# Transposing 42 activation tiles by VectorE blocks and small transfers instead of TensorE, in a decoder layer on one Trainium2 core

## The chip, the core and the metric

The kernel runs on one core of one Trainium2 chip (trn2). The core's engines are TensorE (PE in the rows: matrix products and transposes, results in PSUM), VectorE (DVE), ScalarE (ACT), GpSimd (POOL) and SyncE (SP, which here only issues DMAs). The metric is the time on the device for one execution, in microseconds (us).

## The reference

One hybrid decoder layer and a last norm, in float32, on 256 tokens of width 2048; the inner width of the MLP is 5632.

```
h = rms_norm(x)
qa, ka, va, qb, kb, vb, ga, gb = split(h @ w_in)          # 1024 columns each, ga and gb 2048
oa = differential_attention(rope(qa), rope(ka), va)       # 8 heads, two softmax maps each
ob = stick_breaking_attention(qb, kb, vb)                 # 8 heads
m  = sigmoid(ga) * (oa @ w_proj_a) + sigmoid(gb) * (ob @ w_proj_b)
x  = x + m @ w_out
x  = x + cross_attention(rms_norm(x), rms_norm(mem))      # 4 heads, 256 memory tokens
u  = causal_conv3(rms_norm(x) @ w_up) + bias              # width 2 * 5632, a filter per column
x  = x + (silu(u[gate]) * u[value]) @ w_down
out = rms_norm(x)
```

## The kernel before

Every product is computed in units of 512 columns: x (256 tokens, two blocks of 128) times a [2048 x 512] piece of a weight matrix. The activations stand on TensorE's stationary side, so they are needed with features on the partitions, while a product comes out with tokens on the partitions. What a unit gives therefore has to be transposed before the next matrix can use it.

A weight piece comes from DRAM in four transfers of 1 MB, called b0 to b3 here (`product`, issued on SyncE; three buffers, pool `wr`). Each transfer is worked in two halves of two 128-row blocks, so a unit has halves 0 to 7. For each half ScalarE rounds the weights to a high part (`split_w`, the cast of line 162) and VectorE subtracts it to get the low part (line 163); three buffers each hold these parts. Each 128-row block then takes three matmuls of 128x512 per token block (lines 168, 169, 170: high times high, with the low part of the weights, with the low part of the activations), 12 matmuls a half and 96 a unit. SyncE waits before an issue until VectorE has read the buffer's last content.

Other work is put between the halves. A generator handed to `spawn(gen, delay)` starts `delay` halves later, and `tick()`, once a half, moves waiting generators on; a `yield n` lets n halves pass. SyncE's instructions stay in the order in which the program writes them (`manual_schedule`); on the other engines a scheduler sets the order.

The stages in order: the input projection in 20 units (qa0, ka0, va0, qa1, ka1, va1, then qb0, kb0, vb0, qb1, kb1, vb1, and eight gates), with the attention of a group of heads between the halves of later units; four times a unit of pa and one of pb (1024 rows each, so two transfers each), whose merged result is mT; four units of the output projection (wo, x1T); cross-attention (kx, qx, vx); four short units wxo (512 rows, one transfer each, x2T); 22 units up with the convolution and the gate between their halves; the down projection.

Transposes that the change touches are 42 sets of eight 128x128 transposes on TensorE against an identity, into PSUM. Eight are in `proj_T` (qaT, kaT, qbT, kbT, two of each; qa and ka are rotated on GpSimd first), four in mT, four in x1T, four in x2T (`transposed`), and 22 in `gated` (uT). In the up stage ScalarE scales the unit's two PSUM tiles into `zu` (line 588), and two halves later the transposes and the convolution follow.

Of the kernel before, what the change touches and what calls it, by code (L numbers as in the profile page):

```python
# [9 lines left out]
F32 = mybir.dt.float32  # L10
F32R = mybir.dt.float32r
AF = mybir.ActivationFunctionType
# [5 lines left out]
S = 256          # tokens  # L18
NT = S // P      # token blocks
D = 2048  # L20
KD = D // P      # 128-row blocks of the model width
FF = 5632
KF = FF // P
U = 512          # columns of one product unit
KB = 4           # 128-row blocks per weight transfer
# [6 lines left out]
# columns of the packed per-partition parameters  # L32
# [13 lines left out]
def hybrid_layer(ctx: ExitStack, tc: tile.TileContext, x, xT, mem, memT, gmix, par, gfin,  # L46
# [28 lines left out]
    # additive masks of the diagonal blocks: [q, k] -> 0 where k <= q (k < q), else NEG  # L75
# [8 lines left out]
    # Work that is emitted between the products: generators that yield the number of  # L84
    # half blocks of weights to let pass before they go on.
# [27 lines left out]
    def split(dst, src, gains=None):  # L113
        """dst[:, 0] + dst[:, 1] = src, or src * gain, in two parts of 12 bits.
        dst [P, 2, 2, S], src [P, 2, S]; gains: a [P, 1] column per 128-row block."""
        if gains is None:
            nc.scalar.copy(out=dst[:, 0], in_=src)
            nc.vector.tensor_tensor(out=dst[:, 1], in0=src, in1=dst[:, 0].bitcast(F32),
                                    op=ALU.subtract)
            return  # L120
        for j in range(2):
            nc.scalar.activation(out=dst[:, 0, j], in_=src[:, j], func=AF.Copy, scale=gains[j])
            nc.vector.scalar_tensor_tensor(out=dst[:, 1, j], in0=src[:, j], scalar=gains[j],
                                           in1=dst[:, 0, j].bitcast(F32),
                                           op0=ALU.mult, op1=ALU.subtract)

    def transposed(dst, src, n, name, gains=None):
        """dst: act tiles of the 4 row blocks n*4.. of the transpose; src [P, NT, U]."""
# [11 lines left out]

    def sumsq(dst, src):
        junk = wk.tile([P, U], F32, tag="w2", name="junk")
        nc.scalar.activation(out=junk[:, :src.shape[-1]], in_=src, func=AF.Square, accum_out=dst)

    def rstd(ss, n, width, name):
        """(sum over the last axis of ss [P, n, m] / width + EPS) ** -0.5 -> [P, n]"""
# [19 lines left out]
    def mm3(out, a, b, start=True, stop=True):  # L166
        """out (+)= (a[0] + a[1]).T @ (b[0] + b[1]) without the product of the two low parts."""
# [9 lines left out]
    def product(xs, w, u, kt_n, name, pieces=None, before=None, heap=False):  # L177
        """x @ w[:, unit u] for both token blocks -> two PSUM tiles [P, U].
        pieces: 128-row blocks per transfer; before(kt): called ahead of the transfer from kt on."""
# [25 lines left out]
    def load_split(src, gains, i, name):  # L205
        """Split act tile i of a transposed input [P, KD, S] in DRAM, scaled by gains."""
# [27 lines left out]
    def proj_T2(ps, r, name):  # L234
        """Evacuate a unit scaled by r and transpose it: act tiles of heads 0, 1 and 2, 3."""
# [7 lines left out]
    def proj_T(ps, r, name, rotate=False):  # L243
        """Evacuate a unit scaled by r and transpose it: [P (dim), 4 (head), S]."""
# [9 lines left out]
        def rest():  # L254
            for t in range(NT):
                pt = sm_tile(f"{name}_tp")
                for h in range(4):
                    nc.tensor.transpose(out=pt[:, h * P:(h + 1) * P],
                                        in_=zs[t][:, h * P:(h + 1) * P], identity=ident)
                nc.vector.tensor_copy(out=dst[:, :, t * P:(t + 1) * P],  # L260
                                      in_=pt.rearrange("p (h s) -> p h s", h=4))
            yield 0
        spawn(rest(), 2)
        return dst

    def proj_n(ps, r, name):
        """Evacuate a unit scaled by r: [P (token), NT, U]."""
# [5 lines left out]
    def attn_T(a, name):  # L273
        """Causal weights of one head [q block][P, K] -> [P (key), 3 * P]:
        keys 0 for both query blocks, then keys 1 for query block 1."""
# [8 lines left out]
    # differential attention  # L284
    oaT = [None] * 4

    def diff_head(h):
        qT, kT, v, hh = qa[h // 4], ka[h // 4], va[h // 4], h % 4
        # scores of the two maps, in a bank each: query block 0 in 0:P, query block 1 in P:3 * P
# [62 lines left out]
    # stick-breaking attention, two heads at a time  # L352
    obT = [None] * 4

    def stick_pair(g):
        aw = [[], []]
        for i in range(NT):
# [14 lines left out]
            # softplus(z) = max(z, 0) + ln(1 + exp(-|z|)), zero where masked  # L372
# [27 lines left out]
    # the input projection in units; the attention of a group of heads runs between the products  # L400
# [21 lines left out]
    # lam = exp(q1.k1) - exp(q2.k2) + LAM_INIT, negated, on all partitions  # L422
# [33 lines left out]
    # branch projections, gated and merged  # L456
    mT = [None] * 8
    for n in range(4):
# [9 lines left out]
        spawn(transposed(mT, ga, n, f"mT{n}"), 2)  # L468
# [6 lines left out]
    # output projection and residual  # L475
# [14 lines left out]
    for n in range(4):  # L490
# [4 lines left out]
        spawn(transposed(x1T, xr[n], n, f"x1T{n}", lambda k: col("g_x", k)), 2)  # L495
# [51 lines left out]
    for n in range(4):  # L547
        residual(product(oxT, w_xo, n, 4, f"wxo{n}"), xr[n], n, ss2)
        spawn(transposed(x2T, xr[n], n, f"x2T{n}", lambda k: col("g_ffn", k)), 2)
    r2 = rstd(ss2, NT, D, "r2")  # L550

# [1 line left out]
    gT = [None] * (KF // 2)  # L553

    def gated(i, z):
        us = []
        for part in range(2):          # gate, value
            pt = sm_tile("uT").rearrange("p (j s) -> p j s", j=2)
            for j in range(2):
                for t in range(NT):  # L560
                    c = (2 * part + j) * P
                    nc.tensor.transpose(out=pt[:, j, t * P:(t + 1) * P], in_=z[t][:, c:c + P],  # L562
                                        identity=ident)
            u = wk.tile([P, 2, S], F32, tag="w2", name="u")
            for j in range(2):
                f = part * KF + 2 * i + j
                tap = lambda k: col("cw", k * 2 * KF + f)
                nc.scalar.activation(out=u[:, j], in_=pt[:, j], func=AF.Identity, scale=tap(2),
                                     bias=col("cb", f))
                nc.vector.scalar_tensor_tensor(out=u[:, j, 1:], in0=pt[:, j, 0:S - 1], scalar=tap(1),  # L570
                                               in1=u[:, j, 1:], op0=ALU.mult, op1=ALU.add)
                nc.vector.scalar_tensor_tensor(out=u[:, j, 2:], in0=pt[:, j, 0:S - 2], scalar=tap(0),
# [11 lines left out]
    for i in range(KF // 2):  # L584
        ps = product(x2T, w_up, i, KD, f"up{i}")
        z = [wk.tile([P, U], F32, tag="w2", name=f"zu{t}") for t in range(NT)]
        for t in range(NT):
            nc.scalar.activation(out=z[t], in_=ps[t], func=AF.Copy, scale=r2[:, t:t + 1])
        spawn(gated(i, z), 2)
# [16 lines left out]
    def finish(ps, t):  # L606
        """The last unit's residual, the norm and the store of token block t."""
# [17 lines left out]
    # last unit: token block 0 runs ahead of token block 1, so that its end overlaps products  # L625
# [23 lines left out]
def _weight(w, np):  # L649
    """[K, N] -> [N / U, K / (KB * P), P, KB * U]: one contiguous transfer per block."""  # L650
# [5 lines left out]
def _tokens(a, np):  # L656
    """[S, D] -> [D / U, P, NT, U]"""
# [3 lines left out]
def _features(a, np):  # L661
    """[S, D] -> [P, KD, S]"""
# [49 lines left out]
```

## Time and profile before

| what | value |
|---|---|
| median of 3 runs | 1521.37 us (1520.65 to 1521.76) |
| span of the profiled execution | 1518.9 us |
| TensorE busy | 1503.4 us, 99% of the span |
| VectorE busy | 896.7 us, 59% |
| ScalarE busy | 784.7 us, 52% |
| GpSimd busy | 53.7 us, 4% |
| DMA, main queue | 286.13 MB, 54.5% of 16 engines' span |

The busy time of an engine is the sum over its instructions in one profiled execution; its share is taken of the span, the time from the first to the last instruction. The time of a run is a little longer than the span.

### The profile page before, as it was taken

To read this page: it belongs to the slowest core of one execution; us is meant where nothing else is said; L and a number is where in the kernel's file an instruction comes from. 1 tells how busy PE (TensorE), PEld (TensorE's weight loads), DVE (VectorE), ACT (ScalarE), POOL (GpSimd) and SP (SyncE) were. 2 spreads that over 40 slices of the span, in tenths; PEclk is the share of its full clock that TensorE was granted. 3 is DMA by queue.
4 is the path that set the end of the run, shared out by engine and by line. 5 is a ranking of instruction groups with operands and counts; after the bars stand their busy time and mean duration, and the time that the engine had idled before them with its cause. 6 is when DMAs were issued, how large, how long until landed. Compare 5 with 4: busy or idle time off the path is not lost.

```text
span 1518.9 us, 17599 instructions
## 1 busy us (share of the span) xinstructions
PE 1503.4 (99%) x6904; PEld 1243.2 (82%) x6904; DVE 896.7 (59%) x1131; ACT 784.7 (52%) x1074; POOL 53.7 (4%) x72
## 2 busy tenths in 40 slices
PE   8999999999999999999999999999999999999997
PEld 6878788888888888888888888888888888888886
DVE  5575666564444565664666667666666666444562
ACT  6454555465555344664565555555555555344441
POOL 0202000000000010000000000000000000000010
PEclk9999999999999999999999999999999999999999
DMA  9544444445555556755355555555555555655561
GB/s 349 187 159 152 162 166 167 167 166 194 194 194 193 183 193 246 265 197 192 139 191 174 189 194 178 183 194 185 179 191 192 174 190 192 222 194 192 197 230 73
DMA packets 44003, 287.78 MB, mean 189 GB/s; under 512 B 5008, under 2 KB 5008, under 8 KB 11152
## 3 DMA queue, kind: packets, MB, share of 16 engines
q1 hardware_dynamic: 43488, 286.13, 54.5%
q8 instruction: 54, 0.88, 0.2%
q10 hardware_dynamic: 432, 0.53, 0.1%
q14 instruction: 29, 0.24, 0.0%
HBM read 284.54 MB, written 2.10 MB: 189 GB/s over the span
## 4 chain that ended last, share of the span: by engine, by line
PE 98%; issue 1%; DMA 0%; DVE 0%; ACT 0%; SPq 0%; POOLq 0%; POOL 0%; DVEq 0%
PE up_mm L170 11%; PE up_mm L169 11%; PE up_mm L168 11%; PE dn_mm L168 5%; PE dn_mm L170 5%; PE dn_mm L169 5%; PE g_mm L168 4%; PE g_mm L169 4%; PE g_mm L170 4%; PE wo_mm L170 2%; PE wo_mm L168 2%; PE wo_mm L169 2%; PE uT L562 1%; PE va_mm L169 1%; PE qb_mm L169 1%; PE qb_mm L168 1%
## 5 line engine op out<-in xcount | busy, mean ns | idle before, releaser
L163 DVE TENSOR_TENSOR up_lo<-up_raw,up_hi 128x1024 fp32r<-128x1024 f32 x176 | 215.7, 1226 | 170.3 <-ACT up_hi L162 167.8
L162 ACT CAST up_hi<-up_raw 128x1024 fp32r<-128x1024 f32 x176 | 185.5, 1054 | 197.5 <-PE up_mm L170 176.5
L170 PE MATMUL up_mm<-up_hi,x2T 128*128 128x512 f32 x704 | 274.1, 389 | 0.0
L169 PE MATMUL up_mm<-up_lo,x2T 128*128 128x512 f32 x704 | 274.0, 389 | 0.0
L168 PE MATMUL up_mm<-up_hi,x2T 128*128 128x512 f32 x704 | 254.8, 392 | 0.0
L163 DVE TENSOR_TENSOR dn_lo<-dn_raw,dn_hi 128x1024 fp32r<-128x1024 f32 x88 | 109.9, 1253 | 101.0 <-ACT dn_hi L162 95.7
L170 PEld LDWEIGHTS up_mm<-up_hi,x2T 128*128 128x128 f32 x704 | 132.2, 188 | 27.4
L169 PEld LDWEIGHTS up_mm<-up_lo,x2T 128*128 128x128 f32 x704 | 132.3, 188 | 26.7
L168 PEld LDWEIGHTS up_mm<-up_hi,x2T 128*128 128x128 f32 x704 | 132.2, 188 | 26.6
L162 ACT CAST dn_hi<-dn_raw 128x1024 fp32r<-128x1024 f32 x88 | 92.0, 1056 | 118.0 <-PE dn_mm L170 103.7
L170 PE MATMUL dn_mm<-dn_hi,gT 128*128 128x512 f32 x352 | 136.9, 389 | 0.0
L169 PE MATMUL dn_mm<-dn_lo,gT 128*128 128x512 f32 x352 | 136.9, 389 | 0.0
L163 DVE TENSOR_TENSOR g_lo<-g_raw,g_hi 128x1024 fp32r<-128x1024 f32 x64 | 78.4, 1225 | 83.8 <-ACT g_hi L162 83.8
L168 PE MATMUL dn_mm<-dn_hi,gT 128*128 128x512 f32 x352 | 126.3, 389 | 0.0
L162 ACT CAST g_hi<-g_raw 128x1024 fp32r<-128x1024 f32 x64 | 67.3, 1053 | 73.4 <-PE g_mm L170 70.2
L169 PE MATMUL g_mm<-g_lo,hT 128*128 128x512 f32 x256 | 100.0, 391 | 0.0
L170 PE MATMUL g_mm<-g_hi,hT 128*128 128x512 f32 x256 | 99.8, 390 | 0.0
L168 PE MATMUL g_mm<-g_hi,hT 128*128 128x512 f32 x256 | 90.7, 391 | 0.0
L170 PEld LDWEIGHTS dn_mm<-dn_hi,gT 128*128 128x128 f32 x352 | 66.1, 188 | 13.8
L169 PEld LDWEIGHTS dn_mm<-dn_lo,gT 128*128 128x128 f32 x352 | 66.1, 188 | 13.7
L168 PEld LDWEIGHTS dn_mm<-dn_hi,gT 128*128 128x128 f32 x352 | 66.1, 188 | 13.6
L170 PEld LDWEIGHTS g_mm<-g_hi,hT 128*128 128x128 f32 x256 | 48.1, 188 | 10.0
(301 smaller groups left out, 2664.5 us busy)
## 6 DMA issues: line engine op xcount, KB each, us to landing
up_raw<-in_w_up SPq DMA_DIRECT2D x88, 1024.0 KB, 4.9
dn_raw<-in_w_dn SPq DMA_DIRECT2D x44, 1024.0 KB, 4.9
g_raw<-in_w_in SPq DMA_DIRECT2D x32, 1024.0 KB, 5.0
wo_raw<-in_w_out SPq DMA_DIRECT2D x16, 1024.0 KB, 5.0
ka_raw<-in_w_in SPq DMA_DIRECT2D x8, 1024.0 KB, 6.1
va_raw<-in_w_in SPq DMA_DIRECT2D x8, 1024.0 KB, 5.0
qb_raw<-in_w_in SPq DMA_DIRECT2D x8, 1024.0 KB, 4.9
kb_raw<-in_w_in SPq DMA_DIRECT2D x8, 1024.0 KB, 4.9
```

What stands on the lines that cost most here:

```text
L162: nc.scalar.copy(out=hi, in_=src)
L163: nc.vector.tensor_tensor(out=lo, in0=src, in1=hi.bitcast(F32), op=ALU.subtract)
L168: nc.tensor.matmul(out, lhsT=a[0], rhs=b[0], start=start, stop=False)
L169: nc.tensor.matmul(out, lhsT=a[0], rhs=b[1], start=False, stop=False)
L170: nc.tensor.matmul(out, lhsT=a[1], rhs=b[0], start=False, stop=stop)
L562: nc.tensor.transpose(out=pt[:, j, t * P:(t + 1) * P], in_=z[t][:, c:c + P], identity=ident)
```

## The change

Each of the 42 sets is replaced. `turn` is one VectorE instruction for each token block: it transposes 128x512 values in blocks of 32x32, so that each block is turned but stands where it stood. `regroup` then carries the blocks to their places: 16 DMAs from SBUF to SBUF, one for each pair of a source and a target group of 32 partitions, each of 32 partitions x 8 x 32 values (32 KB in 256 pieces of 128 bytes). All 672 are issued on SyncE. A DMA of a regroup also waits for the DMA eight before it.

The result lies in SBUF rather than in PSUM. In the up stage the scaled unit stays in its PSUM tile (ScalarE works in place), the turns read it there, `gated` starts five halves after the unit and waits three more between its regroup and the convolution. In `flipped` (mT, x1T, x2T) the turns are written at once, the regroup two halves later, the split two more. In `proj_T` the turns come one half later and the regroup three more. Transposes in the attention itself and in the cross-attention stay on TensorE.

```diff
+    def turn(blk, src, t):
+        nc.vector.transpose(out=blk[:, :, t * P:(t + 1) * P], in_=src.rearrange("p (f c) -> p f c", c=P))
+
+    def regroup(dst, blk):
+        q = P // 4
+        d, s = (v.rearrange("p f (t c) -> p (f t) c", t=NT) for v in (dst, blk))
+        for a in range(4):
+            for b in range(4):
+                nc.sync.dma_start(out=d[b * q:(b + 1) * q, :, a * q:(a + 1) * q],
+                                  in_=s[a * q:(a + 1) * q, :, b * q:(b + 1) * q])
...
+    def flipped(dst, src, n, name, gains=None):
+        blk = flip_tile(name)
+        for t in range(NT):
+            turn(blk, src[:, t], t)
+        yield 2
+        z = chunk_tile(f"{name}_z", [P, U // P, S])
+        regroup(z, blk)
+        yield 2
+        for h in range(2):
+            k0 = 4 * n + 2 * h
+            dst[k0 // 2] = act_tile(f"{name}_{h}")
+            split(dst[k0 // 2], z[:, 2 * h:2 * h + 2], None if gains is None else [gains(k0), gains(k0 + 1)])
+        yield 0
...
         def rest():
+            blk = flip_tile(name)
             for t in range(NT):
-                pt = sm_tile(f"{name}_tp")
-                for h in range(4):
-                    nc.tensor.transpose(out=pt[:, h * P:(h + 1) * P],
-                                        in_=zs[t][:, h * P:(h + 1) * P], identity=ident)
-                nc.vector.tensor_copy(out=dst[:, :, t * P:(t + 1) * P],
-                                      in_=pt.rearrange("p (h s) -> p h s", h=4))
-            yield 0
-        spawn(rest(), 2)
+                turn(blk, zs[t], t)
+            yield 3
+            regroup(dst, blk)
+        spawn(rest(), 1)
...
-        spawn(transposed(mT, ga, n, f"mT{n}"), 2)
+        spawn(flipped(mT, ga, n, f"mT{n}"), 0)
...
-        spawn(transposed(x1T, xr[n], n, f"x1T{n}", lambda k: col("g_x", k)), 2)
+        spawn(flipped(x1T, xr[n], n, f"x1T{n}", lambda k: col("g_x", k)), 0)
...
-        spawn(transposed(x2T, xr[n], n, f"x2T{n}", lambda k: col("g_ffn", k)), 2)
+        spawn(flipped(x2T, xr[n], n, f"x2T{n}", lambda k: col("g_ffn", k)), 0)
...
-    def gated(i, z):
+    def gated(i, blk):
+        uT = chunk_tile("uT", [P, U // P, S])
+        regroup(uT, blk)
+        yield 3
         us = []
-        for part in range(2):          # gate, value
-            pt = sm_tile("uT").rearrange("p (j s) -> p j s", j=2)
-            for j in range(2):
-                for t in range(NT):
-                    c = (2 * part + j) * P
-                    nc.tensor.transpose(out=pt[:, j, t * P:(t + 1) * P], in_=z[t][:, c:c + P],
-                                        identity=ident)
...
-        z = [wk.tile([P, U], F32, tag="w2", name=f"zu{t}") for t in range(NT)]
-        for t in range(NT):
-            nc.scalar.activation(out=z[t], in_=ps[t], func=AF.Copy, scale=r2[:, t:t + 1])
-        spawn(gated(i, z), 2)
+        blk = flip_tile(f"up{i}")
+        for t in range(NT):
+            nc.scalar.activation(out=ps[t], in_=ps[t], func=AF.Copy, scale=r2[:, t:t + 1])
+            turn(blk, ps[t], t)
+        spawn(gated(i, blk), 5)
```

The order of instructions on the engines changes with it. First SyncE in the mixer, before the change; a row is an instruction of one line with what it writes and reads, x4 is four of them in sequence, and `kb_raw` is the buffer that receives weights for kb.

```order
L190 DMA qb_raw<-in_w_in 128x2048 x4
L190 DMA kb_raw<-in_w_in 128x2048 x4
L190 DMA vb_raw<-in_w_in 128x2048 x4
L190 DMA qb_raw<-in_w_in 128x2048 x4
L190 DMA kb_raw<-in_w_in 128x2048 x4
```

The same place after the change; line 222 is what line 190 was, line 138 is `regroup`.

```order
L222 DMA qb_raw<-in_w_in 128x2048 x4
L222 DMA kb_raw<-in_w_in 128x2048 x2
L138 DMA qbT_1708<-qbT_blk 32x8x32 x16
L222 DMA kb_raw<-in_w_in 128x2048 x2
L222 DMA vb_raw<-in_w_in 128x2048 x2
L138 DMA kbT_1925<-kbT_blk 32x8x32 x16
L222 DMA vb_raw<-in_w_in 128x2048 x2
L222 DMA qb_raw<-in_w_in 128x2048 x4
L222 DMA kb_raw<-in_w_in 128x2048 x2
L138 DMA qbT_2310<-qbT_blk 32x8x32 x16
L222 DMA kb_raw<-in_w_in 128x2048 x2
```

A regroup of 16 DMAs now stands between b1 and b2 of the following unit. In wo (x1T) it stands there too; va0 has two of them, those of qaT0 and kaT0. In the up stage it stands between b2 and b3 of the following unit (five weight issues, 16, four, 16, four and so on). SyncE at the merged product reads as follows, after the change:

```order
L222 DMA pa_raw<-in_w_pa 128x2048 x2
L222 DMA pb_raw<-in_w_pb 128x2048 x2
L222 DMA pa_raw<-in_w_pa 128x2048 x2
L138 DMA mT_z<-mT_blk 32x8x32 x16
L222 DMA pb_raw<-in_w_pb 128x2048 x2
L222 DMA pa_raw<-in_w_pa 128x2048 x2
L138 DMA mT_z<-mT_blk 32x8x32 x16
L222 DMA pb_raw<-in_w_pb 128x2048 x2
```

Before the change nothing stood between those pa and pb issues; now the regroup of one merged block stands ahead of both issues of the next pb unit.

VectorE in one unit of the up stage, before the change: `up_lo` is the split of a half, 570 and 572 are the convolution's taps, 577 and 578 the gate's products, 118 the split of its result.

```order
L163 TENSOR_TENSOR up_lo<-up_raw,up_hi 128x1024 x5
L570 SCALAR_TENSOR_TENSOR u<-uT,pc,u 128x255 x2
L572 SCALAR_TENSOR_TENSOR u<-uT,pc,u 128x254 x2
L163 TENSOR_TENSOR up_lo<-up_raw,up_hi 128x1024
L570 SCALAR_TENSOR_TENSOR u<-uT,pc,u 128x255 x2
L572 SCALAR_TENSOR_TENSOR u<-uT,pc,u 128x254 x2
L163 TENSOR_TENSOR up_lo<-up_raw,up_hi 128x1024
L577 TENSOR_TENSOR u<-u 128x512
L578 TENSOR_TENSOR sg<-u,sg 128x512
```

And after the change, from the two turns of a unit (line 129):

```order
L129 STREAM_TRANSPOSE up_blk<-up_mm_8376 128x4x128
L129 STREAM_TRANSPOSE up_blk<-up_mm_8377 128x4x128
L195 TENSOR_TENSOR up_lo<-up_raw,up_hi 128x1024 x4
L597 SCALAR_TENSOR_TENSOR u<-uT,pc,u 128x255 x2
L599 SCALAR_TENSOR_TENSOR u<-uT,pc,u 128x254
L597 SCALAR_TENSOR_TENSOR u<-uT,pc,u 128x255
L599 SCALAR_TENSOR_TENSOR u<-uT,pc,u 128x254
L597 SCALAR_TENSOR_TENSOR u<-uT,pc,u 128x255
L599 SCALAR_TENSOR_TENSOR u<-uT,pc,u 128x254 x2
L604 TENSOR_TENSOR u<-u 128x512
L195 TENSOR_TENSOR up_lo<-up_raw,up_hi 128x1024
L605 TENSOR_TENSOR sg<-u,sg 128x512
```

The turns stand between the splits of the next unit's halves 1 and 2. All eight taps now stand together after the split of half 5, where before they lay in two groups with a split between them.

## Rows read from the trace of the kernel before

**Rows 1.** The page: busy times, granted clock in 40 slices, chain by engine.

```profile
PE 1503.4 (99%) x6904; PEld 1243.2 (82%) x6904; DVE 896.7 (59%) x1131; ACT 784.7 (52%) x1074; POOL 53.7 (4%) x72
...
PEclk9999999999999999999999999999999999999999
...
PE 98%; issue 1%; DMA 0%; DVE 0%; ACT 0%; SPq 0%; POOLq 0%; POOL 0%; DVEq 0%
```

**Rows 2.** Timeline, TensorE around a set: start, duration (us), engine, line, operation.

```profile
798.93 0.39 PE L170 MATMUL up_mm<-up_hi,x2T 128*128 128x512 f32 x1
...
799.17 1.03 PE L562 MATMUL uT<-ident,zu 128*128 128x128 f32 x8
...
799.96 0.48 PE L168 MATMUL up_mm<-up_hi,x2T 128*128 128x512 f32 x1
...
800.27 0.40 PE L169 MATMUL up_mm<-up_lo,x2T 128*128 128x512 f32 x1
```

**Rows 3.** Groups by line: busy us, mean ns of one, idle time before.

```profile
L163 DVE TENSOR_TENSOR up_lo<-up_raw,up_hi 128x1024 fp32r<-128x1024 f32 x176 | 215.7, 1226 | 170.3 <-ACT up_hi L162 167.8
L162 ACT CAST up_hi<-up_raw 128x1024 fp32r<-128x1024 f32 x176 | 185.5, 1054 | 197.5 <-PE up_mm L170 176.5
```

**Rows 4.** Timeline, TensorE and ScalarE around the end of an up unit.

```profile
815.70 0.39 PE L168 MATMUL up_mm<-up_hi,x2T 128*128 128x512 f32 x1
...
816.38 0.39 PE L168 MATMUL up_mm<-up_hi,x2T 128*128 128x512 f32 x1
...
815.89 1.37 ACT L588 ACTIVATE zu<-up_mm,r 128x512 f32<-128x512 f32 x2 [0.93 <-PE up_mm L170]
817.16 1.04 ACT L162 CAST up_hi<-up_raw 128x1024 fp32r<-128x1024 f32 x1
819.29 1.06 ACT L162 CAST up_hi<-up_raw 128x1024 fp32r<-128x1024 f32 x1 [1.09 <-PE up_mm L170]
```

**Rows 5.** Timeline, SyncE's issues there: start, time the issue held it.

```profile
811.36 0.33 SPq L190 DMA_DIRECT2D up_raw<-in_w_up  x1
...
816.25 0.33 SPq L190 DMA_DIRECT2D up_raw<-in_w_up  x1
```

**Rows 6.** DMA issues: count, KB each, median us from issue to landing.

```profile
up_raw<-in_w_up SPq DMA_DIRECT2D x88, 1024.0 KB, 4.9
...
out<-xr SPq DMA_DIRECT2D x6, 256.0 KB, 2.3
```

**Rows 7.** Timeline, SyncE's first issues, one behind the other.

```profile
2.59 0.43 SPq L190 DMA_DIRECT2D qa_raw<-in_w_in  x1
3.06 0.43 SPq L208 DMA_DIRECT2D hT_raw<-in_xT  x1
3.54 0.67 SPq L190 DMA_DIRECT2D qa_raw<-in_w_in  x1
```

**Rows 8.** Timeline, merging on VectorE and GpSimd, and a rotation on GpSimd.

```profile
511.19 1.28 DVE L466 TENSOR_TENSOR gate<-pb_mm,gate 128x512 f32<-128x512 f32 x2
...
512.01 3.53 POOL L467 TENSOR_TENSOR gate<-gate,gate 128x512 f32<-128x512 f32 x2 [300.94 <-issue]
...
43.21 1.03 POOL L227 TENSOR_TENSOR rope_a<-qaT_z,pc 128x128 f32<-128x128 f32 x1 [1.01 <-ACT qaT_z L249]
...
47.43 0.46 POOL L232 TENSOR_TENSOR qaT_z<-rope_a,rope_b 128x128 f32<-128x128 f32 x1
```

**Rows 9.** Windows (length, busy times, granted clock, DMA share, GB/s) and two early matmuls.

```profile
52.60:310.00 257.40, 257.40 (x1234) 208.71 (x1233) 159.44 (x264) 129.59 (x230) 19.25 (x32) 1.00 0.48 164
...
1509.90:1513.50 3.60, 0.00 (x0) 0.00 (x0) 2.14 (x5) 1.45 (x3) 0.55 (x1) 1.00 0.00 0
...
1514.00:1518.90 4.90, 0.00 (x0) 0.00 (x0) 0.00 (x0) 0.00 (x0) 0.00 (x0) 0.50 0.51 186
...
7.40 0.63 PE L169 MATMUL qa_mm<-qa_lo,hT 128*128 128x512 f32 x1
7.83 0.63 PE L170 MATMUL qa_mm<-qa_hi,hT 128*128 128x512 f32 x1
```

More of the change, by code (lines that the diff above doesn't have):

```diff
@@ L125, in split, with flip_tile @@
                                            op0=ALU.mult, op1=ALU.subtract)
+    def turn(blk, src, t):
[7 more added lines that the diff above has]
+                                  in_=s[a * q:(a + 1) * q, :, b * q:(b + 1) * q])
+    def flip_tile(name):
+        return chunk_tile(f"{name}_blk", [P, U // P, S])
     def transposed(dst, src, n, name, gains=None):
@@ L566, in gated @@
                 f = part * KF + 2 * i + j
+                z = uT[:, 2 * part + j]
                 tap = lambda k: col("cw", k * 2 * KF + f)
-                nc.scalar.activation(out=u[:, j], in_=pt[:, j], func=AF.Identity, scale=tap(2),
+                nc.scalar.activation(out=u[:, j], in_=z, func=AF.Identity, scale=tap(2),
                                      bias=col("cb", f))
-                nc.vector.scalar_tensor_tensor(out=u[:, j, 1:], in0=pt[:, j, 0:S - 1], scalar=tap(1),
+                nc.vector.scalar_tensor_tensor(out=u[:, j, 1:], in0=z[:, 0:S - 1], scalar=tap(1),
                                                in1=u[:, j, 1:], op0=ALU.mult, op1=ALU.add)
-                nc.vector.scalar_tensor_tensor(out=u[:, j, 2:], in0=pt[:, j, 0:S - 2], scalar=tap(0),
+                nc.vector.scalar_tensor_tensor(out=u[:, j, 2:], in0=z[:, 0:S - 2], scalar=tap(0),
                                                in1=u[:, j, 2:], op0=ALU.mult, op1=ALU.add)
```

## The prediction

> **What bounds the kernel now.** I read the page first: its busy shares, its clock row and its chain of waits [rows 1]. TensorE is busy for 1503.4 of 1518.9 us, holds its clock in every slice, and is 98% of the chain that ended last; VectorE (59%) and ScalarE (52%) have room. So any instruction taken from TensorE pays in full, and so does any moment in which it lacks a split weight. The profiled execution spans 1518.9 us against a median of 1521.37, so about 2.5 us lie outside the span.
>
> Next I read one unit of the up projection as a clockwork. Two matmul starts three steps apart are 815.70 and 816.38 [rows 4], so one step is 0.227 us, a half (12 matmuls) 2.72 and a unit (96) 21.75. Call the end of a unit on TensorE T0; here T0 = 816.38, when the next unit's first matmul starts. Weights arrive as four 1 MB transfers b0 to b3, two halves each. The next unit's b2 is issued at 811.36, T0-5.0, and its b3 at 816.25, T0-0.1 [rows 5]; a transfer takes 4.9 us to land [rows 6]. This early issue is the kernel's only cushion: three buffers, each issue waiting for VectorE to have read the last user.
>
> **What is removed.** A set of eight TensorE transposes starts at 799.17; the last matmul before it started at 798.93, the next two at 799.96 and 800.27 [rows 2]. Without it they would have started at 799.16 and 799.38, so a set costs 0.89 us. There are 42 sets (8 of queries and keys, 4 merged, 8 of the residual stream, 22 up): 42 x 0.89 = 37.4 us less on TensorE. If nothing else happened, the span would be 1481.5.
>
> **What is added on VectorE and ScalarE.** Two turns a set. No row shows one; the nearest are VectorE operations over 128x512, two in 1.28 us [rows 8], and two ScalarE evacuations in 1.37 [rows 4]. I take 0.69 each, with half and twice of it as bounds: the upper end would add 1.4 us to each wait below, some 20 us outside the up stage and 23 in it, the lower take half of the 20. 84 x 0.69 = 58 us are spread over an engine that is 41% idle. In the up stage the turns hang on the evacuations, which start at T0-0.5 [rows 4]: evacuated at T0+0.2 and T0+0.9, turned by about T0+1.6. VectorE is free then: the split of the next half waits for its cast at 817.16 [rows 4]. Hidden.
>
> **What is added on SyncE.** This decides. Each set now has 16 DMAs of 32 KB, 672 in all, in the queue that issues the weights, in program order. They cannot start before the turn, and **the weight block written behind them can't be issued before the last of them**. In the up stage that block is b3, in most other units b2, with the merged sets b0 of the next pb product, four halves after T0 too.
>
> *Price of an issue.* Rows of large issues that follow each other stand 0.47 and 0.48 us apart (2.59, 3.06, 3.54), each busy 0.43; the next one, with the queue filling, holds 0.67 [rows 7]. A single issue is busy 0.33 [rows 5]. None has 256 pieces of 128 bytes. I take 0.46 apart, 0.33 as the lower end, 0.68 as the upper; 16 cost 7.4 us (5.3 to 10.9). Each DMA also waits for the one eight before it; the nearest small landing is 2.3 us [rows 6], which allows eight in 2.3 us or 0.29 each and so does not bind first.
>
> *What a delay costs.* If b2 is issued at T0+W, it lands at W+4.9; cast (1.05) and split (1.23) [rows 3] stand before its first half, of which a little overlaps, as the first product needs the cast alone: 2.0 together. Half 4 is wanted at T0 + 4 x 2.72 = T0+10.9. **Stall = W - 4.0.** For b3, wanted at T0 + 6 x 2.72 = 16.3, the stall is W - 9.4. In mixer units attention runs in between: ten units took 257.4 us [rows 9] against 217.5 for their halves, 4.0 a unit with 0.7 of it removed transposes; half of the 3.3 falls before half 4, so there the stall is W - 5.6.
>
> *Up stage, 22 sets.* W = 1.65 + 7.4 = 9.05, just inside 9.4. The last piece lands near 1.65 + 15 x 0.46 + 2.3 = 10.9; ScalarE has the convolution between the casts of halves 5 and 6, so the cast of half 6 (needed by about T0+14) can slip a few tenths. I put 0.2 us on each: 5 us. It is an edge: every further 0.1 us of pitch adds 1.6 us to W, and 35 us to the stage.
>
> *Mixer, 8 sets.* vb0 and vb1 carry kbT; VectorE turns it straight after the evacuation, so W = 9.05 and the stall 3.5 each: 7. va0 and va1 wait for the rotation on GpSimd, which starts at 43.21 and ends at 47.89 for two blocks [rows 8], 4.7 us after an evacuation at T0+0.9, then 0.7 for the second turn: W = 13.7, stall 8 each: 16. In ka1, kb0 and kb1 the order puts the turns behind the split of half 3 and behind copies of attention results; half 3's cast starts at 819.29 [rows 4], its split ends some 2.3 later, T0+5.2, two turns T0+6.6, W = 14.0, stall 8.4 for one and some 10 where a copy of TensorE's result stands between: about 28. Some attention work moves in front of half 4 and fills part of this; I take 3 off. Sum 48.
>
> *Merged, 4 sets.* VectorE takes up the product of pb at 511.19, half a us before its end as in the up stage, so T0 = 511.7; GpSimd's adds end at 512.01 + 3.53 = 515.54 [rows 8], T0+3.9; the second turn ends at T0+4.7; W = 12.1, stall 8.1: 32. *First residual, 4 sets.* Two adds as long as those (1.28 from T0-0.5), two turns: T0+2.2; W = 9.6, stall 5.6, the first unit 1.2 more for two other DMAs: 24. *Second residual, 4 sets.* Here b0 to b3 of the short wxo units and the first up blocks stand between the sets; the same sum gives 5.8, 3.1, 1.6 and 2.4: 13. Together 48 + 32 + 24 + 13 = 117 us.
>
> *Clock.* From 1509.9 on TensorE has no work left; the record holds 1.00 to 1513.5, and from 1514 it shows 0.50 [rows 9], the lower of its two levels. Thirteen of these stalls pass 4 us. After its first wait TensorE stepped by 0.43 (7.40 to 7.83 [rows 9]) instead of 0.227, for some seven steps: 1.4 us. 13 x 1.4 = 18.
>
> **A rule against a row.** The issue rows hold SyncE for 0.33 to 0.67 us [rows 5, 7], and 16 pieces of 32 KB are together half of a 1 MB transfer that lands in 4.9 [rows 6]; so the issues, at 7.4 us, outlast the bytes. The Trainium skill, DMA: Bandwidth & Descriptors, section "Issuing engines are not separate DMA queues", calls the time a sequencer takes to initiate a DMA "usually small relative to the DMA itself". The rows disagree here; by the rule a set would hold the queue for little more than one landing, which is rival C below.
>
> **Sum.** 1518.9 - 37.4 + 5 + 117 + 18 = 1621.5, with 2.5 outside the span 1624.
>
> **Rivals.** *B, the up stage stalls too.* At a pitch of 0.68, W grows by 3.5: in the up stage 9.05 + 3.5 - 9.4 = 3.15 x 22 = 69; outside it some 15 places x 3.5 = 53 more; 1624 - 5 + 69 + 53 = 1741, more where a slower turn or further drops of the clock join. For it: the queue's filling row, and 256 pieces each; against it: the steady pitch of 0.47. From a pitch of 0.5 on it decides.
> *C, faster.* Issuing is so cheap that W is little more than the turn and one landing, 2.3 + about 0.4 instead of 7.4. Then each stall shrinks by 4.7: the mixers to about 18, merged 13, residuals 7, no clock loss worth naming: 1518.9 - 37.4 + 38 + 2.5 = 1522, no change; it turns faster only where the cushion is also 1 to 2 us larger than my T0+4.0 (15 places x 1.5 = 22): about 1500. It needs a pitch under 0.1, and no row here is under 0.33.
> *D, the low end.* At 0.33 the stalls outside are 117 - 15 x 2.1 = 85, none in the up stage, clock 12: 1518.9 - 37.4 + 97 + 2.5 = 1581.
>
> **How the numbers follow.** A measurement of this kernel can tell about 0.2%, 3 us, from no change. My forecast, stalls at the sets outside the up stage with the up stage near its edge (1550 to 1690, with D in it): 0.63. B, above 1690: 0.25. C: 0.12, of which faster 0.08 and no change 0.04. The time is 1624; the range 1550 to 1790 leaves out C and the upper third of B.
>
> **What would show it.** Right: TensorE's busy time falls by 37 us while its idle time rises to over 130; the releasers of that idle time are casts of b2 and b0 blocks in the mixer, merged and residual stages, and behind them SyncE issuing line 138; windows over the gates (which have no sets) and the down projection keep their length; a unit of the up projection takes 22.0 us. Each step: issues of line 138 stand 0.46 us apart; b2 goes out 9 to 14 us after T0; a turn takes 0.7; the granted clock falls after the long stalls. Wrong: a pitch far from 0.46 (the up stage tells first), a turn over 1.4 us, or weights that land well after 4.9 us because 128-byte pieces hold the DMA engines.

## The result and the profile after

The changed kernel takes 1836.89 us (1836.44 to 1841.31), against 1521.28 for the kernel before: a ratio of 1.2082, with 1.2068 to 1.2097. It is slower, as forecast, but by 316 us where I had 103, and the time lies above my range. The profiled execution spans 1834.9 us.

The page of the changed kernel, busy times, granted clock and the chain that ended last; these answer to [rows 1].

```profile
PE 1570.2 (86%) x6568; PEld 1259.7 (69%) x6568; DVE 944.5 (51%) x1199; ACT 787.0 (43%) x1074; POOL 52.7 (3%) x72
...
PEclk9897989899999878888988899999999999999999
...
PE 28%; SPq 17%; DMA 9%; DVE 4%; ACT 3%; issue 2%; POOL 0%; ACTq 0%; POOLq 0%; DVEq 0%
SPq L138 17%; DMA up_raw<-in_w_up 7%; PE dn_mm L201 4%; PE dn_mm L202 4%; PE dn_mm L200 4%; PE up_mm L201 3%; PE up_mm L202 3%; PE up_mm L200 3%; DVE up_blk L129 2%; ACT up_hi L194 1%; DMA wo_raw<-in_w_out 1%; DVE up_lo L195 1%; PE wo_mm L200 1%; PE wo_mm L201 1%; ACT up_mm L615 1%
```

The shares of the chain are of the whole span, and here the chain could be followed back only to 667.8 us, so they add up to 63%. Of this, TensorE, which had 98% before, holds 28. SyncE, which computes nothing, holds 17 by line 138 alone, the issues of the small DMAs. TensorE has 336 instructions fewer and is nevertheless busy for 67 us longer: its granted clock is below 9 tenths in 13 of the 40 slices. Two things were lost, waiting time and clock.

Where, by stages, in the windows view of the changed kernel (from one stage's first matmul to the next one's: input projection with attention, gates, merge, output projection, cross-attention, up, down). After the length and the busy times of PE, PEld, DVE, ACT and POOL stand the granted clock, the DMA share and GB/s.

```profile
0.00:392.00 392.00, 318.50 (x1370) 252.40 (x1371) 195.73 (x314) 163.34 (x286) 23.35 (x53) 0.90 0.47 159
392.00:571.00 179.00, 179.00 (x808) 148.63 (x807) 85.28 (x78) 92.34 (x101) 0.00 (x0) 1.00 0.55 188
571.00:700.50 129.50, 96.42 (x385) 76.75 (x384) 56.77 (x59) 38.49 (x41) 10.63 (x6) 0.86 0.41 138
700.50:837.80 137.30, 97.28 (x385) 76.67 (x384) 61.07 (x79) 53.96 (x90) 3.55 (x2) 0.85 0.52 180
837.80:963.60 125.80, 102.83 (x457) 83.76 (x457) 65.57 (x95) 56.08 (x93) 2.17 (x2) 0.91 0.45 140
963.60:1578.30 614.70, 530.91 (x2103) 419.62 (x2104) 355.45 (x459) 281.17 (x354) 1.59 (x1) 0.92 0.53 172
1578.30:1834.90 256.60, 245.22 (x1067) 201.85 (x1065) 124.68 (x118) 101.59 (x113) 11.43 (x8) 0.98 0.53 186
```

The same stages of the kernel before, cut in the same way.

```profile
0.00:310.00 310.00, 303.53 (x1429) 246.10 (x1430) 189.49 (x309) 163.43 (x285) 26.18 (x53) 1.00 0.54 188
310.00:489.70 179.70, 179.70 (x813) 149.15 (x812) 88.83 (x84) 93.01 (x102) 0.00 (x0) 1.00 0.55 187
489.70:579.60 89.90, 89.90 (x409) 74.44 (x408) 52.80 (x53) 38.78 (x41) 10.61 (x6) 1.00 0.57 193
579.60:670.40 90.80, 90.80 (x418) 75.39 (x418) 57.20 (x71) 54.49 (x90) 3.54 (x2) 1.00 0.71 249
670.40:770.90 100.50, 100.50 (x488) 84.39 (x487) 61.47 (x84) 55.49 (x90) 1.36 (x2) 1.00 0.49 168
770.90:1269.40 498.50, 498.50 (x2291) 414.85 (x2290) 324.85 (x419) 279.15 (x358) 0.69 (x1) 1.00 0.55 186
1269.40:1518.90 249.50, 240.46 (x1065) 198.91 (x1064) 122.09 (x115) 100.31 (x112) 11.36 (x8) 0.99 0.53 186
```

The gates, which have no sets, keep their 179 us. The up stage grew by 116, the input projection by 82, merge 40, output projection 47, cross-attention with the second residual 25. The down projection was to keep its length and is 7 us longer: the regroup of the last up unit falls into it, and TensorE waits there for 3.4 us.

One up unit of the changed kernel in the timeline; its end on TensorE, T0, is near 1030.0.

```profile
1029.49 1.34 ACT L615 ACTIVATE up_mm<-up_mm,r 128x512 f32<-128x512 f32 x2 [1.35 <-PE up_mm L202]
1030.18 1.40 DVE L129 STREAM_TRANSPOSE up_blk<-up_mm 128x512 f32<-128x512 f32 x2 [0.78 <-ACT up_mm L615]
...
1031.64 11.37 SPq L138 DMA_DIRECT2D uT<-up_blk  x16
...
1043.12 9.71 SPq L222 DMA_DIRECT2D up_raw<-in_w_up  x4
1044.58 2.08 ACT L595 ACTIVATE u<-uT,pc 128x256 f32<-128x256 f32 x4 [5.66 <-DMA uT<-up_blk]
...
1048.44 1.99 ACT L194 CAST up_hi<-up_raw 128x1024 fp32r<-128x1024 f32 x2 [0.34 <-DMA up_raw<-in_w_up]
```

The reader sees the chain of the prediction row by row. The turns end at T0+1.6, as worked out; the 16 issues take 11.4 us; b3 goes out at 1043.12, T0+13.1, instead of T0-0.1 [rows 5]; it lands 5.2 us later and the cast starts at once. TensorE, in the same unit:

```profile
1045.61 0.39 PE L202 MATMUL up_mm<-up_hi,x2T 128*128 128x512 f32 x1
1049.53 0.73 PE L200 MATMUL up_mm<-up_hi,x2T 128*128 128x512 f32 x2 [3.54 <-ACT up_hi L194]
1050.79 0.67 PE L201 MATMUL up_mm<-up_lo,x2T 128*128 128x512 f32 x1 [0.53 <-DVE up_lo L195]
...
1053.82 0.63 PE L200 MATMUL up_mm<-up_hi,x2T 128*128 128x512 f32 x1
...
1054.54 0.40 PE L202 MATMUL up_mm<-up_hi,x2T 128*128 128x512 f32 x1
```

And the windows of that place:

```profile
1046.00:1049.50 3.50, 0.00 (x0) 0.00 (x0) 3.25 (x8) 2.36 (x5) 0.00 (x0) 1.00 1.00 424
...
1052.00:1054.00 2.00, 2.00 (x6) 1.52 (x6) 2.00 (x3) 0.50 (x1) 0.00 (x0) 0.50 0.60 164
...
1056.00:1058.00 2.00, 2.00 (x11) 1.64 (x10) 1.23 (x1) 0.57 (x2) 0.00 (x0) 1.00 0.27 115
```

Behind a wait of 3.54 us the clock is granted at 0.50, the lower level: the 2 us from 1052 touch 6 matmuls, the 2 us from 1056, at 1.00, touch 11. This wait is paid for twice.

The lines view of the small DMAs and the turns (durations in ns, least, median and most):

```profile
L138 SPq DMA_DIRECT2D uT<-up_blk x352: 586/609/1880, 1002.8 to 1592.5; - x176
...
L129 DVE STREAM_TRANSPOSE up_blk<-up_mm x44: 695/717/718, 1001.4 to 1581.9; 128x512 f32<-128x512 f32 x44
```

An issue holds SyncE for 0.609 us, and with the gap behind it the 16 stand 0.65 apart (10.4 us for 16 in half of the sets, up to 11.7 in the others). The turn, at 0.717, is where I had put it.

### The profile page after: what moved, and what is told of

The parts are those of the page before. It is cut to its first block, busy times and chain, and to the rows that moved or that the text cites. A ratio compares the mean times of both kernels' runs of the same rounds, so it can differ in the third digit from the quotient of the medians.

```text
span 1834.9 us, 17957 instructions
## 1 busy us (share of the span) xinstructions
PE 1570.2 (86%) x6568; PEld 1259.7 (69%) x6568; DVE 944.5 (51%) x1199; ACT 787.0 (43%) x1074; POOL 52.7 (3%) x72
## 4 chain that ended last, share of the span: by engine, by line
PE 28%; SPq 17%; DMA 9%; DVE 4%; ACT 3%; issue 2%; POOL 0%; ACTq 0%; POOLq 0%; DVEq 0%
SPq L138 17%; DMA up_raw<-in_w_up 7%; PE dn_mm L201 4%; PE dn_mm L202 4%; PE dn_mm L200 4%; PE up_mm L201 3%; PE up_mm L202 3%; PE up_mm L200 3%; DVE up_blk L129 2%; ACT up_hi L194 1%; DMA wo_raw<-in_w_out 1%; DVE up_lo L195 1%; PE wo_mm L200 1%; PE wo_mm L201 1%; ACT up_mm L615 1%
## 5 line engine op out<-in xcount | busy, mean ns | idle before, releaser
L200 PE MATMUL up_mm<-up_hi,x2T 128*128 128x512 f32 x704 | 258.3, 412 | 79.0 <-ACT up_hi L194 79.0
L201 PE MATMUL up_mm<-up_lo,x2T 128*128 128x512 f32 x704 | 294.6, 418 | 8.9 <-DVE up_lo L195 8.7
L202 PE MATMUL up_mm<-up_hi,x2T 128*128 128x512 f32 x704 | 290.5, 413 | 0.0
L200 PEld LDWEIGHTS up_mm<-up_hi,x2T 128*128 128x128 f32 x704 | 139.1, 201 | 118.2 <-ACT up_hi L194 89.2
L201 PEld LDWEIGHTS up_mm<-up_lo,x2T 128*128 128x128 f32 x704 | 142.3, 202 | 51.8 <-DVE up_lo L195 21.7
L202 PEld LDWEIGHTS up_mm<-up_hi,x2T 128*128 128x128 f32 x704 | 142.5, 202 | 30.0
L595 ACT ACTIVATE u<-uT,pc 128x256 f32<-128x256 f32 x88 | 45.8, 591 | 110.3 <-DMA uT<-up_blk 110.3
L597 DVE SCALAR_TENSOR_TENSOR u<-uT,pc,u 128x255 f32<-128x255 f32 x88 | 42.3, 481 | 96.8 <-ACT u L595 96.6
L200 PE MATMUL wo_mm<-wo_hi,mT 128*128 128x512 f32 x128 | 48.4, 420 | 39.9 <-ACT wo_hi L194 39.9
L200 PEld LDWEIGHTS dn_mm<-dn_hi,gT 128*128 128x128 f32 x352 | 66.6, 189 | 17.2 <-ACT dn_hi L194 3.3
```

The costliest lines, as they stand in the source:

```text
L200: nc.tensor.matmul(out, lhsT=a[0], rhs=b[0], start=start, stop=False)
L201: nc.tensor.matmul(out, lhsT=a[0], rhs=b[1], start=False, stop=False)
L202: nc.tensor.matmul(out, lhsT=a[1], rhs=b[0], start=False, stop=stop)
L595: nc.scalar.activation(out=u[:, j], in_=z, func=AF.Identity, scale=tap(2), bias=col("cb", f))
L597: nc.vector.scalar_tensor_tensor(out=u[:, j, 1:], in0=z[:, 0:S - 1], scalar=tap(1), in1=u[:, j, 1:], op0=ALU.mult, op1=ALU.add)
```

## The experiments

Three theories were set against each other. **Q**: the issues of the small DMAs hold the weight block that is queued behind them on SyncE. **U**: the convolution on ScalarE waits for the last piece, and a cast waits behind it. **T**: 128-byte pieces load the DMA engines, so weights land late.

**no_regroup: the small DMAs left out.** Consumers read the turned blocks where they stand; the output is not the reference's.

```diff
-        z = chunk_tile(f"{name}_z", [P, U // P, S])
-        regroup(z, blk)
+        z = blk
...
-                turn(blk, zs[t], t)
-            yield 3
-            regroup(dst, blk)
+                turn(dst, zs[t], t)
+            yield 0
...
-        uT = chunk_tile("uT", [P, U // P, S])
-        regroup(uT, blk)
+        uT = blk
```

> All 672 small DMAs are left out; what follows reads the turned blocks where they stand, so blocks are in the wrong places in every later product. Turns, evacuations and all else stay. Theory Q, and T as well: no stalls are left, 1481 to 1492. A rival that puts cost on the turns (VectorE late, or PSUM held longer): above 1500.

Measured: 1482.33 us. From its page, and from the windows view over its up stage:

```profile
PE 1466.1 (99%) x6568; PEld 1208.0 (82%) x6568; DVE 935.2 (63%) x1199; ACT 781.5 (53%) x1074; POOL 56.1 (4%) x72
...
751.60:1233.00 481.40, 481.32 (x2123) 398.20 (x2122) 355.71 (x472) 280.58 (x363) 3.13 (x1) 1.00 0.57 195
```

TensorE is busy for 37.3 us less than before; 37.4 was the estimate for 42 sets. The turns, the evacuation in PSUM and the later convolution cost nothing. All 354 us between this and the changed kernel come with the DMAs.

**up_late: the regroup of the up stage behind b3.**

```diff
-        spawn(gated(i, blk), 5)
+        spawn(gated(i, blk), 7)
```

> In the up stage alone the regroup is written after b3 of the following unit instead of ahead of it. Theory Q (the 16 issues, 0.65 us apart, hold the weight block behind them on SyncE): the block behind is now b0 of the unit after next, which has some 14.8 us from the end of a unit; 1.65 + 10.4 = 12.1 is inside. An up unit goes from 28.0 to about 22 us, the total from 1837 to 1695-1715. Rival U (the cast of half 6 stands behind the convolution on ScalarE, which waits for the last piece): little changes, since the convolution still waits on ScalarE, 1800-1840. Rival T (the 128-byte pieces load the DMA engines, so weights land late: 6.1 us instead of 4.9): the traffic is the same, so the up unit stays above 26 us, 1790-1840.

Measured: 1720.91 us, 116 less. The edit moves one group of issues behind one weight block; it moves the convolution as well, which u_later, below, does alone and to no effect. The up stage takes 505 us (from its first matmul at 964.9 to the down projection's at 1470.0) instead of 615. SyncE there, with the regroup between b3 and the next b0, and below it the windows view of 390 us of this stage:

```profile
1049.83 10.40 SPq L138 DMA_DIRECT2D uT<-up_blk  x16
1060.35 10.03 SPq L222 DMA_DIRECT2D up_raw<-in_w_up  x4
1071.91 10.40 SPq L138 DMA_DIRECT2D uT<-up_blk  x16
...
1010.00:1400.00 390.00, 384.82 (x1681) 313.90 (x1680) 275.38 (x363) 218.66 (x279) 0.00 (x0) 1.00 0.65 208
```

As many issues, as long, repeating every 22.08 us, and TensorE is idle for 5.2 of the 390 us from 1010 to 1400. T is out as the main cause: the traffic is the same, and the weights still land in a median of 5.9 us (6.1 in the changed kernel). The total is 6 us above the band of Q; three waits of 3.5 to 4.1 us at the start of the stage, behind the sets of x2T, are not touched by this edit.

**u_later: the convolution two halves later, the regroup where it was.**

```diff
         regroup(uT, blk)
-        yield 3
+        yield 5
```

> In the up stage the convolution is put two halves later, the regroup stays ahead of b3. Theory Q: b3 is as late as before, an up unit stays at 27-28 us, total 1810-1840. Rival U: with the convolution out of the way of the cast of half 6 the stall of some 4 us and the clock lost behind it go, 22 us a unit, 1700-1720.

Measured: 1834.92 us, 2 us less than the changed kernel: no change worth naming. U is refuted: ScalarE's 5.7 us of waiting in the timeline above are hidden behind the same late b3.

**long_pieces: the same bytes in 32 pieces of 1 KB.** The values land in wrong places.

```diff
-                nc.sync.dma_start(out=d[b * q:(b + 1) * q, :, a * q:(a + 1) * q],
-                                  in_=s[a * q:(a + 1) * q, :, b * q:(b + 1) * q])
+                nc.sync.dma_start(out=dst[b * q:(b + 1) * q, a],
+                                  in_=blk[a * q:(a + 1) * q, b])
```

> Each of the 16 DMAs moves the same 32 KB, but as 32 pieces of 1 KB instead of 256 of 128 bytes (values land in wrong places, so the output differs). If the time of an issue goes by its pieces, it falls from 0.61 to the 0.33-0.43 of the other issues, 16 take 6 to 7.5 us instead of 10.4, and the total goes to about 1590-1640, near what I had forecast. If it goes by the instruction, 0.6 us each stay and the total is 1820-1840. Rival T alone, with issues unchanged, would show landing of weights at 4.9 and 1780-1820.

Measured: 1781.63 us. The lines view:

```profile
L137 SPq DMA_DIRECT2D uT<-up_blk x352: 507/589/1772, 991.1 to 1539.4; - x176
```

With an eighth of the pieces an issue is 0.02 us shorter. It does not go by pieces. The total lies in the band of T, but its sign is missing: the weights of the up stage land in a median of 5.8 us, not 4.9 (6.1 in the changed kernel), and b3 alone in 5.1 (5.4). So the length of the pieces has a small part in the landing at most. The 55 us gained are more than 16 x 0.02 a set explains. In the up stage, 41 us shorter, 26 are shorter waits and 15 are clock: it falls behind 12 of the 22 up sets, where in the changed kernel it falls behind all of them. This edit also lets a part of the convolution start when the first DMAs have landed. What shortens the waits was not taken apart.

**four_issues: four DMAs of 128 partitions and 128 KB.** The values land in wrong places.

```diff
-        for a in range(4):
-            for b in range(4):
-                nc.sync.dma_start(out=d[b * q:(b + 1) * q, :, a * q:(a + 1) * q],
-                                  in_=s[a * q:(a + 1) * q, :, b * q:(b + 1) * q])
+        for a in range(4):
+            nc.sync.dma_start(out=dst[:, a], in_=blk[:, (a + 1) % 4])
```

> Each regroup is 4 DMAs of 128 partitions and 128 KB instead of 16 of 32 partitions and 32 KB; the same bytes, values in wrong places. If an issue costs by the instruction (0.61 us whatever it moves), a regroup holds SyncE for 2.6 us. By the sums of the prediction with 16c = 2.6: none in the up stage, mixers some 18, merged 13, first residual 4, second 3, so 1518.9 - 37.4 + 38 + 2.5 and a few us of clock, 1515 to 1530. If it costs by bytes or partitions, 4 issues take as long as 16 did, and the time stays near 1780 to 1840.

Measured: 1546.54 us, against 1515 to 1530. The lines view of its small DMAs, and the busy times of its page:

```profile
L135 SPq DMA_DIRECT2D uT<-up_blk x88: 470/592/601, 842.0 to 1300.8; - x88
...
PE 1488.4 (96%) x6568; PEld 1218.9 (79%) x6568; DVE 937.7 (61%) x1199; ACT 787.9 (51%) x1074; POOL 51.9 (3%) x72
```

Four times the bytes and partitions, and an issue still takes 0.592 us: the price is one of the instruction. The run is 290 us faster than the changed kernel. Its pieces are 1 KB long, as in long_pieces, so it is the 235 us against that run that a quarter of the issues brings. TensorE is idle for 1544.8 - 1488.4 = 56.4 us, 41 over the kernel before, where the sum gave 38. What I missed is 1488.4 - 1466.1 = 22 us of busy time, at the lower clock: "a few us of clock" was again too little.

**filler: work for TensorE in the wait.** 14 matmuls with a zero matrix, added to the same sums, ahead of half 6 of each up unit.

```diff
+                if name.startswith("up") and k0 + h == 12:
+                    for f in range(14):
+                        nc.tensor.matmul(ps[f % 2], lhsT=zr, rhs=xs[0][:, 0].rearrange("p c s -> p (c s)"),
+                                         start=False, stop=False)
```

> The changed kernel, with 14 more matmuls (a zero matrix, 3.2 us) on TensorE ahead of half 6 of each up unit, where it waits for some 3.5 to 4 us; they add zero to the same sums. If the waits cost more than their length because the granted clock falls behind them, the clock stays up and a unit goes from 28.0 to about 25.7: 1780 to 1795. If the clock falls for another reason (the transfers' load, say), 1830 to 1845; if the matmuls simply come on top, 1890 to 1910.

Measured: 1805.66 us: 308 matmuls more, and 31 us less. The windows view over its up stage:

```profile
967.00:1551.30 584.30, 564.82 (x2420) 454.71 (x2421) 356.29 (x460) 282.26 (x354) 1.59 (x1) 0.99 0.56 182
```

The granted clock of the stage rises from 0.92 to 0.99, and a unit goes from 27.9 to 26.6 us. The record shows three falls in this stage, all behind sets of x2T, and none behind the up stage's own sets. So the clock did fall because of the wait. That it gained 31 and not 42 to 57 has to do in part with the filler itself: waits of 0.2 to 0.7 us stayed behind it, and the waits behind x2T, 8 us in this stage, have no filler.

**pool_later: all small DMAs issued by GpSimd, the work that reads them later.**

```diff
-                nc.sync.dma_start(out=d[b * q:(b + 1) * q, :, a * q:(a + 1) * q],
+                nc.gpsimd.dma_start(out=d[b * q:(b + 1) * q, :, a * q:(a + 1) * q],
...
         regroup(uT, blk)
-        yield 3
+        yield 5
```

> The 672 DMAs are issued by GpSimd, which is busy for 3%, so that no weight issue stands behind them; the work that reads the result is put later (two halves in the up stage, four in the first residual and three merged sets), so that nothing waits in front of a cast. Theory Q: 1485 to 1515, whatever waits remain being those of the attention and of mT3 and x2T. If 16 issues on GpSimd take longer than a unit (over 1.36 us each), GpSimd sets the pace of the up stage and the time goes above 1600.

Measured: 1661.80 us, a miss for Q and for its rival.

```profile
L138 POOL DMA_DIRECT2D uT<-up_blk x352: 582/584/593, 852.4 to 1439.2; - x176
...
1053.02 9.21 POOL L138 DMA_DIRECT2D uT<-up_blk  x16 [20.31 <-issue]
...
1080.35 0.76 PE L200 MATMUL up_mm<-up_hi,x2T 128*128 128x512 f32 x1 [4.71 <-ACT gT L117]
```

GpSimd issues at the same price, 9.2 us a set out of 28, so it does not set the pace, and no weight stands behind it. What TensorE waits for, 12 times for 56 us in all, is now ScalarE's split of the convolution's result (gT), itself late behind the later convolution. The order that the scheduler gave ScalarE and VectorE in this version is the new wait; why the first matmul of a unit needs that instruction I did not settle. With that wait in it, the run neither supports theory Q nor speaks against it.

**spread: SyncE's issues in groups of four, each behind another weight block.** In the up stage it is two groups of eight, from b3 on; kaT and kbT keep 16 together behind b3; mT3 and x2T go back to TensorE.

```diff
-        regroup(uT, blk)
-        yield 3
+        regroup(uT, blk, [0, 1])
+        yield 2
+        regroup(uT, blk, [2, 3])
+        yield 1
...
-        regroup(z, blk)
-        yield 2
+        for a in range(4):
+            regroup(z, blk, [a])
+            yield 2 if a < 3 else 1
```

> A version meant to beat both: SyncE still issues the small DMAs, but in groups of four (of eight in the up stage), each group behind another weight block, from b3 of the following unit on; kaT and kbT keep their 16 together behind b3; mT3 and x2T (5 sets, needed at once) go back to TensorE for 5 x 0.89 = 4.5 us. A group holds a weight block for 2.6 us (5.2 in the up stage) against some 9 of slack, so by theory Q nothing stalls but parts of the attention: 1487 to 1505. If the sum of issue time per unit, not its place, were what counts, it would stay above 1700.

Measured: 1517.79 us (1514.56 to 1521.45), 0.9979 of before (0.9969 to 0.9989). With 592 of the 672 small DMAs left, nearly all of the loss is gone: what decides is where the issues stand and how many stand together, not how many the kernel has. Five sets went back to TensorE here; the waits behind them in the changed kernel, 10.8 us for mT3 and 22.6 for x2T, are a tenth of the 319 us gained. It misses the 1487 to 1505: the input projection with the attention takes 322.5 us where no_regroup has 303.3.

**mixed: spread, with queries and keys on TensorE.** The edit is shown against spread.

```diff
-                turn(blk, zs[t], t)
-            yield 6
...
+                pt = sm_tile(f"{name}_tp")
+                for h in range(4):
+                    nc.tensor.transpose(out=pt[:, h * P:(h + 1) * P],
+                                        in_=zs[t][:, h * P:(h + 1) * P], identity=ident)
```

> The version that spreads its issues, with the eight sets of queries and keys back on TensorE (7.1 us there). In that version the input projection took 19 us more than without small DMAs, and the transposes cost 7.1: theory Q gives 1518 - 19 + 7 = 1506, 1502 to 1511. If those 19 us were not from the eight sets, it gives 1525.

Measured: 1500.88 us, a little under the band. The input projection falls by 12.7 us (322.5 to 309.8), as expected; the up units, whose code is the same, also went from 22.3 to 22.0.

**two_queues: mixed, with SyncE and GpSimd issuing eight each in the up stage.** The edit is shown against mixed.

```diff
-                nc.sync.dma_start(out=d[b * q:(b + 1) * q, :, a * q:(a + 1) * q],
+                eng = nc.gpsimd if a in other else nc.sync
+                eng.dma_start(out=d[b * q:(b + 1) * q, :, a * q:(a + 1) * q],
...
-        regroup(uT, blk, [0, 1])
-        yield 2
-        regroup(uT, blk, [2, 3])
-        yield 1
+        regroup(uT, blk, other=(2, 3))
+        yield 3
```

> As mixed, and in the up stage SyncE issues eight of a set's DMAs and GpSimd the other eight at the same time, behind b3. The last piece lands near 1.65 + 8 x 0.65 + 1.9 = 8.8 us after the end of a unit instead of 17, before ScalarE comes to the convolution. By theory Q an up unit goes from 22.3 to 21.8 us and the total to 1481 + 13 sets x 0.89 + 2 = 1495, with 1493 to 1502. If GpSimd's issues disturb VectorE or the weights' landing, 1506 or more.

Measured: 1497.59 us (1496.81 to 1498.45), 0.9846 of before (0.9833 to 0.9860): 23 us faster than the kernel before.

```profile
1031.43 1.40 DVE L129 STREAM_TRANSPOSE up_blk<-up_mm 128x512 f32<-128x512 f32 x2 [0.42 <-ACT up_mm L623]
...
1032.85 6.50 SPq L139 DMA_DIRECT2D uT<-up_blk  x8
...
1033.12 4.59 POOL L139 DMA_DIRECT2D uT<-up_blk  x8 [17.16 <-DVE up_blk L129]
...
1039.46 13.66 SPq L224 DMA_DIRECT2D up_raw<-in_w_up  x4
...
1043.24 2.08 ACT L603 ACTIVATE u<-uT,pc 128x256 f32<-128x256 f32 x4
...
748.00:1230.00 482.00, 482.00 (x2144) 399.28 (x2142) 353.53 (x463) 283.57 (x371) 93.86 (x163) 1.00 0.68 213
```

Both queues issue side by side, the convolution no longer waits (no idle time is noted before it), and TensorE is busy throughout a window of 482 us, nearly all of it the up stage, at full clock. A unit takes 21.8 us, 0.2 less than in mixed.

## Why the prediction was wrong

**What held.** The removed transposes: 37.4 forecast, 37.3 measured. The turns: 0.69 against 0.717, hidden. The place, in the main: weight blocks behind 16 issues, everywhere outside the gates; the down projection has one such place too, where it was to have none. The landing of a small DMA, 1.9 us, against the 2.3 taken from the output's; it does not bind.

**First step that failed: the price of an issue.** "I take 0.46 apart"; it is 0.65. It was taken from the steady rows of large issues [rows 7], not from the 0.67 row beside them, which I kept for the upper end. (That the queue was filling in that row no run shows.) At 0.65 a set holds SyncE for 10.4 us. My own sums then give 117 + 15 places x 16 x 0.19 = 163 us of waits outside the up stage. Measured: TensorE is idle for 264.7 us after and 15.5 before, 249.2 more, of which 614.7 - 530.9 = 83.8 in the up stage; the other 165.4 answer to the 163. That they come so close is in part luck, for some of them are of a kind that the sums do not have. The waits view of TensorE, over the whole run:

```profile
PE sa L324 <- DMA kaT<-kaT_blk: 12.5, 2, 7.7
...
PE sb L392 <- DMA kbT<-kbT_blk: 5.2, 2, 2.8
```

In the attention the scores wait, for 17.7 us in all, until the turned keys have landed; weight blocks hold the mixers for 40 us, where the sums at 0.65 give 72 (48 + 8 x 16 x 0.19).

In the up stage, "just inside 9.4" became W = 12 to 13.4. The formula's stall is then 2.7 to 4.0 us. Behind its own sets the stage waits 3.6 us in the mean (83.8 without 7.8 behind x2T, over the 21 sets whose stall falls into it). What exceeds the formula at 10.4 us a set is the issues that hold SyncE longer, 11.4 us in the unit shown, and the landing of b3: 5.2 us in that unit and 5.4 in the median, where I had 4.9. (The median of 6.1 over all 88 blocks comes from b0 and b1, which go out within 1.5 us of b3 and land after 7.3 and 9.3.) Of the excess of 213 us in the span (1834.9 - 1621.5), 249.2 - 122 = 127 are waiting, most of it this step: the pitch of 0.65 alone gives 46 outside the up stage and 22 x 2.65 - 5 = 53 in it.

**Second step that failed: the clock.** "Thirteen of these stalls pass 4 us ... 13 x 1.4 = 18." I took the 4 us from the end of the run, where the record holds 1.00 for some 4 us after the last work [rows 9]. The trace of the changed kernel shows the fall behind the wait of each of the 22 up sets, and these waits are 2.5 to 4.4 us long. A fall cost about 2.1 us (530.9 - 481.3 of no_regroup's up stage, by 24 falls, three of them behind x2T), not 1.4. Over the kernel it is 1570.2 - 1466.1 = 104 us instead of 18: the other 86 of the 213. The filler run shows the cause: with work in the wait the clock stays.

**The rivals.** B was the case: the up stage stalls too. I gave it 0.25 and 1741 us. Its waits were close (117 + 53 + 69 = 239 against 249); the clock was left at 18. Its sentence "more where further drops of the clock join" was true and had no number, and the range ended at 1790 for want of one: 1741 + 86 would have been 1827. C needed an issue under 0.1 us; none is under 0.33 anywhere.

**The rule weighed.** The Trainium skill, DMA: Bandwidth & Descriptors, section "Issuing engines are not separate DMA queues", has initiation usually small relative to the DMA. Here an issue takes 0.61 us beside a landing of 1.9, and 16 in one queue take 10.4. It also says that issuing from several engines saves only the sequencer's time; in two_queues that time is what was saved, 0.2 us a unit against mixed, while the larger gains came from the place of the burst in its queue (27.9 to 22.1 us a unit in up_late).

## What to carry to other kernels

When a queue that issues prefetches also gets a burst of small DMAs, count the issues, not the bytes, and ask which prefetch stands behind them in program order. Move the burst behind the block with the most slack, break it up, or share it with an idle engine's queue: with the same 16 issues a unit took 27.9 us in one place, 22.1 in another, and 21.8 with two queues. Price the clock with each wait of TensorE: in the mean of the changed kernel's up stage, 3.8 us of waiting made a unit 6.1 us longer.

## What the runs showed of the hardware

In the four forms tried, an issue of an SBUF to SBUF DMA takes about 0.6 us in the median: 0.609 (32 KB in 256 pieces), 0.589 (32 KB in 32 pieces), 0.592 (128 KB over 128 partitions), 0.584 on GpSimd. Issues with DRAM on one side take 0.33 in the kernel before, 0.43 to 0.67 at its start [rows 7]. What makes the difference (two on-chip addresses, the wait on an earlier DMA that each carries) was not tried.

The clock falls behind shorter waits of TensorE than the end of the run had suggested, and the length of a wait does not tell whether it will. In mixed TensorE waits 2.06 us in one unit of wo, and the clock stays at 1.00:

```profile
645.52 0.50 PE L202 MATMUL wo_mm<-wo_lo,mT 128*128 128x512 f32 x1 [2.06 <-DVE wo_lo L196]
...
645.50:650.50 5.00, 4.98 (x22) 4.12 (x23) 4.11 (x5) 3.02 (x6) 0.00 (x0) 1.00 0.47 146
```

In two_queues it waits as long ahead of the same matmul, and the clock falls:

```profile
646.34 0.79 PE L203 MATMUL wo_mm<-wo_lo,mT 128*128 128x512 f32 x1 [2.06 <-DVE wo_lo L197]
...
646.30:651.30 5.00, 4.96 (x15) 3.99 (x16) 2.85 (x3) 1.97 (x4) 0.00 (x0) 0.66 0.40 139
```

In long_pieces the clock falls behind 12 of the 22 up sets, one with a wait of 1.57 us, and stays behind ten, one with a wait of 2.38; each of these waits has one of 0.53 behind it. So the price of the clock did not begin at the 4 us that one row had suggested. Behind waits of 1.6 to 2.8 us it came in some cases and not in others, and what decides there these runs do not show.
